# Seven products instead of eight in six more stages of a decoder trunk, with one PSUM bank per product

## The chip, the cores and the metric

The kernel runs on one core of a Trainium2 chip. Its time is the device time of one execution in microseconds; three executions before the change took 2046.9, 2049.47 and 2049.53 us, so the median is 2049.47 us. TensorE multiplies matrices into PSUM, VectorE (DVE in the profile) and ScalarE (ACT) do element-wise work, GpSimd (POOL) issues some of the transfers, SyncE (SP) issues the weight loads.

## The reference

One layer of a decoder for 256 tokens of width 2048, all in float32. A hybrid mixer runs three branches of width 1024 on the normalised input: differential attention (8 heads of two maps each), a causal convolution of 31 taps, and a chunked retention. Each branch result goes through its own 1024x2048 matrix, is multiplied by a sigmoid gate that is itself a 2048x2048 product, and the sum goes through `w_out`. Then comes cross-attention of 4 heads into 256 memory tokens (`w_q`, `w_kv`, `w_o`), then a SwiGLU feed-forward of width 5632 (`w_13`, `w_2`), each with a residual, and a last norm.

```python
h = rmsnorm(x, norm_mix)
x = x + hybrid_mixer(h, ...)                 # w_in: 18 blocks for the branches, 12 for the gates
x = x + cross_attention(rmsnorm(x, norm_xattn), rmsnorm(mem, norm_mem), wq, wkv, wo)
x = x + (silu(a) * b) @ w2                   # a, b = split(rmsnorm(x, norm_ffn) @ w13)
```

A block below is 512 output columns for all 256 tokens over the whole inner width; a weight chunk is 256 inner rows by 512 columns, half a megabyte.

## The kernel before

**Products in three parts.** Every weight chunk comes by one transfer from SP into a buffer of `raw` (10 of them). ACT rounds it to the short float format (`wh`, the high part, L198 to L199), DVE subtracts it from the chunk (`wl`, the low part, L201 to L202), and TensorE multiplies high by high, high by low and low by high (L286 to L288). `wh` and `wl` have 5 buffers each; a chunk's work is a unit, and the emitter makes the parts of up to 4 units ahead of the one whose products it emits (`LA`, L290 to L300). A unit of an ordinary block (`block`, L310) is 12 matmuls of 512 columns: two inner tiles, two token halves, three parts.

**The seven-product step.** `pair` (L388) takes two blocks with the same inputs. For the inner chunks marked S it splits the 2x2 arrangement of token halves and weight halves into seven products in place of eight (Strassen's scheme in Winograd's form): `quad_jobs` (L316) makes seven units of 6 matmuls where the ordinary way has four of 12. For this DVE adds weight halves into a raw buffer (`add`), POOL issues two accumulating transfers (L359, L375), and the inputs need four sums, `shi` and `slo`. Four of the seven products go to four PSUM banks of their own (`alloc_tp1`, L329) and are combined in `leave` (L404). Before the change this is used in ten pairs of the feed-forward stage, on two of the four inner chunks, twenty quads in all. The inputs there are normalised beforehand (`normalised`); elsewhere the row scale (`rsx`, `rsm`) is applied when a block leaves PSUM.

**What sets the order.** Attention, convolution, transposes and the like are generators, tasks; `pump` (L129) lets each of them take one step after each unit. Engine queues run in order. Instructions are placed by a scheduler with its own estimate of time, except those issued while `pin[0]` is set (L71 to L84), which keep the order in which the code wrote them, and the weight loads. While a pair's first part runs, `lock` stops all tasks that don't say 2.

Of the kernel before, what the change touches and what calls it, by code (L numbers as in the profile page):

```python
# [33 lines left out]
_CC = {}  # L34
# [6 lines left out]
LA = 4  # L41

# [13 lines left out]
def trunk(ctx, tc, xT, xtok, memT, memtok, w_in, w_br, w_out, w_q, w_kv, w_o, w_13, w_2,  # L56
# [7 lines left out]
    s4 = ctx.enter_context(tc.tile_pool(name="s4", bufs=27))  # L64
    sm = ctx.enter_context(tc.tile_pool(name="sm", bufs=4))
    tiny = ctx.enter_context(tc.tile_pool(name="tiny", bufs=12))
    psm = ctx.enter_context(tc.tile_pool(name="psm", bufs=2, space=bass.MemoryType.PSUM))
    pst = ctx.enter_context(tc.tile_pool(name="pst", bufs=4, space=bass.MemoryType.PSUM))
# [3 lines left out]
    class Pinned:  # L72


        def __init__(self, eng):
            self.eng = eng

        def __getattr__(self, name):
            f = getattr(self.eng, name)

            def g(*a, **k):
                i = f(*a, **k)  # L82
                return tc.keep_in_program_order(i) if pin[0] else i
            return g  # L84

    sc = Pinned(nc.scalar)
    ve = Pinned(nc.vector)
    pe = Pinned(nc.tensor)
# [25 lines left out]
    lock = [False]  # L114

    def spawn(gen):
        active.append(gen)
        return gen

    def step(g):  # L120
        try:
            said[g] = next(g)
# [5 lines left out]

    def pump():  # L129
        for g in list(active):  # L130
            if g in active and (not lock[0] or said.get(g) == 2):
                step(g)

    def drain(g):
        if g in active:
            assert not lock[0]
# [3 lines left out]
    def settle():  # L140

        for g in list(active):
            while g in active and said.get(g) == 1:
# [83 lines left out]
    def alloc_mm(ps):  # L227
# [62 lines left out]
    def emit_unit(i):  # L290
# [4 lines left out]
        for pr in u["prods"]:  # L295
            if pr[1] not in pr[0]:
                u["alloc"](pr[0])
# [18 lines left out]
    def quad_jobs(pp, ps0, ps1, w0, w1, a):  # L316
# [12 lines left out]
        def alloc_tp1(ps):  # L329
            for k in (1, 5, 6, 7):  # L330
                ps[k] = TP()
# [48 lines left out]
        def f4(u):  # L380
            parts(u, t.pop("a"))

        return ([unit(pp, 1, 0, 0, "n", f1, b11=w0[:, 0:2, :]),
                 unit(ps0, 0, 2, 0, "n", f2, b21=b21, b12=w1[:, 0:2, :]), unit(pp, 5, 0, 0, "s", f5),
                 unit(ps1, 0, 0, 3, "s", f3, b22=b22), unit(pp, 6, 0, 1, "s", f6)],
                [unit(pp, 7, 0, 2, "s", f7)], [unit(ps0, 1, 2, 1, "n", f4)])

    def pair(W0, W1, acts, modes, evac0, evac1):  # L388
# [15 lines left out]
        def leave():  # L404
            x0, x1 = S4([P, 2, 512]), S4([P, 2, 512])
            p1, u3, u4, v = x0[:, 0, :], x0[:, 1, :], x1[:, 0, :], x1[:, 1, :]
            sc.copy(p1, pp[1])

            ve.tensor_tensor(out=v, in0=pp[6], in1=p1, op=ALU.subtract)
# [1003 lines left out]
```

## Time and profile before

| | |
|---|---|
| median of three executions | 2049.47 us |
| the profiled execution | 2047.52 us |
| its span, first to last instruction | 2045.5 us |
| TensorE busy | 2021.5 us, 99% |
| VectorE busy | 1372.8 us, 67% |
| ScalarE busy | 1021.8 us, 50% |
| GpSimd busy | 54.8 us, 3% |
| weights and inputs read | 407.69 MB |

The shares are averages over the whole program. The stages differ: in the memory products VectorE is under half busy, in the convolution and attention part and in the feed-forward pairs it is mostly busy. The granted TensorE clock was 0.997 of full speed over the span.

### The profile page before, as it was taken

How to read it: one execution, taken by the hardware profiler on the slowest of the kernel's cores; microseconds unless marked ns; L12 is line 12 of the kernel's file. 1: busy time of each engine (PE TensorE's matmuls, PEld its weight loads, DVE VectorE, ACT ScalarE, POOL GpSimd, SP SyncE). 2: the span in 40 equal slices, each digit the busy share in tenths (PEclk: the TensorE clock that was granted, in tenths of full speed). 3: DMA queues.
4: the chain of work that ended last, by engine and by line, in shares of the span. 5: the costliest groups of instructions: out<-in, count | busy, mean ns of one | idle time of the engine just before them, and what ended most of it. 6: DMA issues, size and time to landing. Idle time of an engine off the chain costs nothing.

```text
span 2045.5 us, 24731 instructions
## 1 busy us (share of the span) xinstructions
PE 2021.5 (99%) x9253; PEld 1669.4 (82%) x9253; DVE 1372.8 (67%) x1684; ACT 1021.8 (50%) x1257; POOL 54.8 (3%) x72
## 2 busy tenths in 40 slices
PE   9999999999999999999999999999999999999998
PEld 6888888888888888888888888878788887888876
DVE  6995699776555556544455555588865888658874
ACT  7444444557544455444445544555543555435553
POOL 0000000000000000000000000000000000000100
PEclk9999999999999999999999999999999999999999
DMA  9656555554565666666655544548866788757881
GB/s 377 205 189 193 176 182 168 175 165 161 181 204 194 225 203 220 213 197 193 202 190 181 164 143 154 179 145 246 251 231 185 229 241 247 241 181 232 240 277 69
DMA packets 113879, 411.40 MB, mean 201 GB/s; under 512 B 12768, under 2 KB 13024, under 8 KB 113760
## 3 DMA queue, kind: packets, MB, share of 16 engines
q1 hardware_dynamic: 105552, 380.46, 54.9%
q0 software_dynamic: 8064, 29.36, 7.3%
q8 instruction: 72, 1.18, 0.2%
q14 instruction: 47, 0.39, 0.1%
q10 hardware_dynamic: 144, 0.01, 0.0%
HBM read 407.69 MB, written 2.10 MB: 200 GB/s over the span
## 4 chain that ended last, share of the span: by engine, by line
PE 84%; issue 6%; DMA 4%; DVE 3%; ACT 1%; POOL 0%; ACTq 0%; SPq 0%; POOLq 0%; DVEq 0%
PE mm L82 77%; PE tp L82 7%; DMA raw<-in_w 4%; DVE wl L82 2%; ACT wh L82 1%; DVE raw L82 1%; DVE s L82 1%; DMA raw<-in_w_in 0%; POOL raw L359 0%; ACT s L82 0%; SPq L90 0%; ACTq L1408 0%; ACTq L82 0%; POOLq L1408 0%; POOL rs L1275 0%
## 5 line engine op out<-in xcount | busy, mean ns | idle before, releaser
L82 PE MATMUL mm<-wh,s 128*128 128x512 f32 x5168 | 1632.0, 392 | 4.2 <-ACT wh L82 3.6
L82 DVE TENSOR_TENSOR wl<-raw,wh 128x1024 fp32r<-128x1024 f32 (+1 forms) x765 | 926.0, 1221 | 585.9 <-ACT wh L82 532.2
L82 ACT CAST wh<-raw 128x1024 fp32r<-128x1024 f32 (+1 forms) x765 | 793.4, 1051 | 831.1 <-PE mm L82 499.1
L82 PEld LDWEIGHTS mm<-wh,s 128*128 128x128 f32 x5168 | 970.0, 188 | 207.3 <-ACT wh L82 5.4
L82 PE MATMUL mm<-wl,s 128*128 128x512 f32 x2584 | 1009.5, 391 | 5.2 <-DVE wl L82 5.2
L82 PEld LDWEIGHTS mm<-wl,s 128*128 128x128 f32 x2584 | 485.9, 188 | 106.3 <-DVE wl L82 8.7
L82 PE MATMUL tp<-wh,s 128*128 128x512 f32 x384 | 130.7, 392 | 0.0
L82 DVE SCALAR_TENSOR_TENSOR s<-s,prm_t,s 128x256 fp32r<-128x256 f32 (+30 forms) x256 | 105.1, 466 | 0.0
L82 PEld LDWEIGHTS tp<-wh,s 128*128 128x128 f32 x384 | 72.7, 189 | 15.2
L82 DVE TENSOR_TENSOR s<-mm,s 128x1024 f32<-128x1024 f32 (+1 forms) x52 | 61.4, 1180 | 24.6 <-PE mm L82 24.6
L82 PE MATMUL tp<-wl,s 128*128 128x512 f32 x192 | 75.2, 392 | 0.0
L82 ACT ACTIVATE s<-s 128x512 f32<-128x512 f32 (+1 forms) x50 | 35.6, 713 | 75.7 <-DVE s L82 75.4
L82 DVE TENSOR_TENSOR s<-tp,s 128x512 fp32r<-128x512 f32 (+1 forms) x102 | 68.0, 685 | 7.3 <-PE tp L82 4.2
L82 DVE TENSOR_TENSOR s<-s,s 128x1024 f32<-128x1024 f32 (+4 forms) x68 | 66.3, 985 | 2.6 <-ACT s L82 1.3
L82 PE MATMUL tp<-cst_t,s 128*128 128x128 f32 x408 | 58.4, 273 | 5.3 <-ACT s L82 5.3
L82 PEld LDWEIGHTS tp<-cst_t,s 128*128 128x128 f32 x408 | 48.7, 140 | 17.5 <-ACT s L82 7.8
L82 PE MATMUL tp<-s,s 128*128 128x256 f32 (+4 forms) x340 | 52.7, 315 | 0.0
L82 PEld LDWEIGHTS tp<-s,s 128*128 128x128 f32 (+1 forms) x340 | 45.1, 189 | 6.4 <-issue 2.1
L82 DVE TENSOR_TENSOR raw<-raw,raw 128x1024 f32<-128x1024 f32 x40 | 48.9, 1222 | 0.6
L82 PEld LDWEIGHTS tp<-wl,s 128*128 128x128 f32 x192 | 36.3, 189 | 7.7
L82 ACT CAST s<-tp 128x512 fp32r<-128x512 f32 x58 | 32.7, 585 | 7.6 <-PE tp L82 7.6
L82 ACT ACTIVATE s<-mm,rsx 128x512 f32<-128x512 f32 x40 | 25.4, 687 | 20.2 <-PE mm L82 20.1
(77 smaller groups left out, 428.3 us busy)
## 6 DMA issues: line engine op xcount, KB each, us to landing
raw<-in_w SPq DMA_DIRECT2D x264, 512.0 KB, 5.1
raw<-in_w_in SPq DMA_DIRECT2D x239, 512.0 KB, 4.5
raw<-in_w_kv SPq DMA_DIRECT2D x64, 512.0 KB, 4.6
raw<-in_w_br SPq DMA_DIRECT2D x48, 512.0 KB, 4.3
raw<-in_w POOLq DMA_DIRECT2D x40, 512.0 KB, 8.3
raw<-in_w_out SPq DMA_DIRECT2D x32, 512.0 KB, 4.7
raw<-in_w_q SPq DMA_DIRECT2D x32, 512.0 KB, 4.2
raw<-in_w_o SPq DMA_DIRECT2D x32, 512.0 KB, 4.0
```

The source lines that it names most:

```text
L82: i = f(*a, **k)
```

## The change

The seven-product step is now used also in the differential-attention projections (three pairs, one S chunk of four, `MODES1`), the gates (six pairs), the memory keys and values (four), `w_out` (two), the last two blocks of `w_o` (one) and `w_2` (four), each with two S chunks of four (`MODES2`): 3 + 17 x 2 = 37 more quads. The block products of retention and the convolution stay ordinary, but take normalised inputs `xn`, as all of `w_in` does after its first two blocks.

The seven products of a pair now run product by product over its quads (p1 of both, p2 and p5 of both, p3 and p6 of both, p7, p4), each finished product leaves its bank at once (`join1` to `join7`), so a pair holds one bank at a time, and tasks run on while a pair runs, as long as no more than 3 banks are held (`cap`). Inside a pair ACT, DVE and TensorE keep the written order. Keys, values and the residual `x2` are parked in DRAM by transfers from POOL and loaded again when needed.

```diff
@@ pump and settle
-            if g in active and (not lock[0] or said.get(g) == 2):
+            if g in active and (said.get(g) or held() + wants[g] <= cap[0]):
                 step(g)
@@ quad_jobs
-        def alloc_tp1(ps):
-            for k in (1, 5, 6, 7):
-                ps[k] = TP()
+        def alloc_tp1(ps, key):
+            ps[key] = TP()
@@ pair
         def enter():
-            for c in sset:
-                need(acts[c])
-            settle()
+            settle(3)
+            cap[0] = 3
             pin[0] = True
-            lock[0] = True
...
+        def join1():
             x0, x1 = S4([P, 2, 512]), S4([P, 2, 512])
...
+            sc.copy(x0[:, 0, :], pp.pop(1))
+
+        def join5():
+            ve.tensor_tensor(out=xs[1][:, 1, :], in0=pp.pop(5), in1=xs[0][:, 0, :], op=ALU.add)
+
+        def join6():
+
+            p = pp.pop(6)
+            ve.tensor_tensor(out=xs[1][:, 0, :], in0=p, in1=xs[1][:, 1, :], op=ALU.subtract)
+            ve.tensor_tensor(out=xs[0][:, 1, :], in0=p, in1=xs[0][:, 0, :], op=ALU.subtract)
+
+        def join7():
+            p = pp.pop(7)
+            ve.tensor_tensor(out=xs[0][:, 1, :], in0=p, in1=xs[0][:, 1, :], op=ALU.subtract)
+            ve.tensor_tensor(out=xs[1][:, 1, :], in0=xs[1][:, 0, :], in1=p, op=ALU.subtract)
+            cap[0] = 4
...
+        first = units_of(("p1",), ("p2", "p5"), ("p3", "p6"))
...
+        us += mixed([marked(i, f) for i, f in enumerate(first)], n0)
+        us += [f() for f in units_of(("p7",))]
+        call(join7)
+        us += mixed(units_of(("p4",)), n1[:len(n1) // 2])
+        call(done(0, ps0, evac0))
         us += [f() for f in n1[len(n1) // 2:]]
+        call(done(1, ps1, evac1))
@@ inputs of the step
+    def factors(a, q):
+
+        f = S4([P, 4, 256])
...
+        for o, x, y, op in ((0, a22, a21, ALU.subtract), (2, a11, a21, ALU.subtract),
+                            (1, a22, fv[:, 2], ALU.add), (3, a12, fv[:, 1], ALU.subtract)):
+            ve.tensor_tensor(out=fv[:, o], in0=x, in1=y, op=op)
+        yield
+        a.shi, a.slo = S4([P, 4, 256], F32R), S4([P, 4, 256], F32R)
+        sc.copy(a.shi, f)
+        ve.tensor_tensor(out=a.slo, in0=f, in1=a.shi.bitcast(F32), op=ALU.subtract)
+
+    def whole(a):
+        q = S4([P, 4, 256])
+        ve.tensor_tensor(out=q, in0=a.hi.bitcast(F32), in1=a.lo.bitcast(F32), op=ALU.add)
+        return q
...
+    def times(q, rb):
+        ve.tensor_tensor(out=q, in0=q, in1=rb[:, None, :].broadcast_to([P, 4, 256]), op=ALU.mult)
@@ stages
+    diff_qk(0)
+    win(4, 5, MODES1, ev_dv(0), lambda ps: dst2[1].update(v=ps))
+    diff_qk(1)
...
+            win(18 + 4 * br + nb, 19 + 4 * br + nb, MODES2, ev_gate(nb), ev_gate(nb + 1))
...
+            pair(w0, w1, mm, MODES2, ev_kv(dst[h]), ev_kv(dst[h + 1]))
...
+        pair(w0, w1, mT, MODES2, ev1(nb), ev1(nb + 1))
...
+    pair(w0, w1, oT, MODES2, ev2(2), ev2(3))
...
+            pair(w0, w1, hT[lo:lo + 4], MODES2, ev_w2(nb), ev_w2(nb + 1))
@@ parking
+        def f(x):
+            nc.gpsimd.dma_start(out=dst, in_=x)
...
+            nc.gpsimd.dma_start(out=x2d[nb], in_=ps)
...
+            x2[nb] = S4([P, 2, 512])
+            nc.gpsimd.dma_start(out=x2[nb], in_=x2d[nb])
```

What moves, in two places. The first is one head of differential attention on DVE. Its score banks are `tp` (two maps), `tn` holds small statistics, the `128x2x128` row adds the causal mask, the last row of each map is the scaled maximum, and `s4_404` is the convolution, which runs beside it. Before:

```order
L82 TENSOR_TENSOR wl_583_3320<-raw_581_3317,wh_582_3319 128x1024
L82 TENSOR_TENSOR tp_566_3243<-tp_566_3243,cst_t_80 128x2x128
L82 TENSOR_TENSOR tp_567_3244<-tp_567_3244,cst_t_80 128x2x128
L82 TENSOR_REDUCE tn_572_3271<-tp_566_3243 128x1 x2
L82 TENSOR_SCALAR tn_572_3271<-tn_572_3271 128x2
L82 TENSOR_REDUCE tn_578_3304<-tp_567_3244 128x1 x2
L82 TENSOR_SCALAR tn_578_3304<-tn_578_3304 128x2
L82 RECIPROCAL tn_584_3337<-tn_571_3269 128x4
```

Now, a head in the third attention pair, on DVE again:

```order
L85 TENSOR_TENSOR tp_623_3427<-tp_623_3427,cst_t_82 128x2x128
L85 TENSOR_REDUCE tn_630_3450<-tp_623_3427 128x1 x2
L85 TENSOR_SCALAR tn_630_3450<-tn_630_3450 128x2
L85 TENSOR_TENSOR wl_633_3458<-raw_585_3235,wh_632_3457 128x1024
L85 SCALAR_TENSOR_TENSOR s4_404_2273<-s4_385_2170,prm_t_81,s4_404_2273 128x239
L85 SCALAR_TENSOR_TENSOR s4_404_2273<-s4_385_2170,prm_t_81,s4_404_2273 128x238
L85 TENSOR_TENSOR tp_624_3428<-tp_624_3428,cst_t_82 128x2x128
L85 TENSOR_REDUCE tn_634_3476<-tp_624_3428 128x1 x2
L85 TENSOR_SCALAR tn_634_3476<-tn_634_3476 128x2
L85 TENSOR_TENSOR wl_637_3484<-raw_577_3191,wh_636_3483 128x1024
```

The two maps of a head, together before, now stand in two successive steps, each followed at once by the low part of a weight chunk. On ACT at the same place stand the two exponentials of a map (`ACTIVATE`, into `sm`) and then the high part that this low part needs:

```order
L85 ACTIVATE sm_631_3454,tn_629_3448<-tp_623_3427,tn_630_3450 128x128
L85 ACTIVATE sm_631_3454,tn_629_3448<-tp_623_3427,tn_630_3450 128x256
L85 CAST wh_632_3457<-raw_585_3235 128x1024
L85 ACTIVATE sm_635_3480,tn_629_3448<-tp_624_3428,tn_634_3476 128x128
L85 ACTIVATE sm_635_3480,tn_629_3448<-tp_624_3428,tn_634_3476 128x256
L85 CAST wh_636_3483<-raw_577_3191 128x1024
```

The high part of the next chunk stands behind the exponentials that read the maximum; nothing else of DVE stands between that maximum and the low part.

The second place is TensorE at the change from one feed-forward pair to the next. `mm_1968` and `mm_2380` are results of a pair, `tp` a product's bank or a transpose's, `s4_1953` and `s4_2353` the gated hidden block of the pair before, which the four 128-column rows transpose. Before, in the later part of the next pair:

```order
L82 MATMUL mm_1968_10812<-wh_1997_10956,s4_1920_10614 128x512
L82 MATMUL mm_1968_10812<-wl_1998_10957,s4_1920_10614 128x512
L82 MATMUL mm_1968_10812<-wh_1997_10956,s4_1921_10615 128x512
L82 MATMUL tp_2014_11027<-cst_t_80,s4_1953_10774 128x128 x4
L82 MATMUL mm_1979_10859<-wh_2000_10968,s4_1954_10779 128x512
```

Now, right at the start of the next pair:

```order
L85 MATMUL mm_2380_11914<-wh_2404_12029,s4_2276_11444 128x512
L85 MATMUL tp_2421_12123<-wh_2407_12047,s4_2231_11256 128x512
L85 MATMUL tp_2421_12123<-wl_2408_12048,s4_2231_11256 128x512
L85 MATMUL tp_2421_12123<-wh_2407_12047,s4_2232_11257 128x512
L85 MATMUL tp_2421_12123<-wh_2407_12047,s4_2231_11256 128x512
L85 MATMUL tp_2421_12123<-wl_2408_12048,s4_2231_11256 128x512
L85 MATMUL tp_2421_12123<-wh_2407_12047,s4_2232_11257 128x512
L85 MATMUL tp_2424_12132<-cst_t_82,s4_2353_11802 128x128 x4
```

The transposes have come forward from after the seventh product of the next pair to after its first unit of six matmuls.

## Rows read from the trace of the kernel before

**Rows 1.** Page: span, busy time and share by engine, instructions.
```profile
span 2045.5 us, 24731 instructions
...
PE 2021.5 (99%) x9253; PEld 1669.4 (82%) x9253; DVE 1372.8 (67%) x1684; ACT 1021.8 (50%) x1257; POOL 54.8 (3%) x72
```
**Rows 2.** Stages: stretch, length, busy (x) PE PEld DVE ACT POOL, clock, DMA, GB/s.
```profile
920.00:980.00 60.00, 60.00 (x266) 49.69 (x265) 27.11 (x23) 26.65 (x28) 0.00 (x0) 1.00 0.60 192
```
**Rows 3.** The same columns: both attention groups, first gate block, second gate block.
```profile
283.60:432.40 148.80, 148.80 (x716) 122.53 (x715) 126.02 (x253) 68.53 (x101) 1.73 (x1) 1.00 0.53 172
432.40:458.30 25.90, 25.90 (x131) 21.13 (x130) 20.06 (x42) 16.34 (x34) 1.64 (x1) 1.00 0.51 164
...
471.80:497.10 25.30, 25.30 (x126) 20.55 (x125) 17.00 (x34) 23.82 (x41) 0.00 (x0) 1.00 0.44 145
```
**Rows 4.** The same columns: three feed-forward pairs.
```profile
1411.20:1454.30 43.10, 42.16 (x189) 34.41 (x188) 37.50 (x35) 23.47 (x26) 3.44 (x4) 1.00 0.79 239
1585.50:1626.30 40.80, 40.80 (x182) 33.78 (x181) 34.09 (x31) 24.02 (x24) 3.45 (x4) 1.00 0.83 246
...
1668.60:1712.60 44.00, 42.33 (x190) 34.45 (x189) 37.51 (x35) 24.13 (x27) 3.45 (x4) 1.00 0.80 239
```
**Rows 5.** VectorE in time: start, length, operation, count.
```profile
1413.46 1.22 DVE L82 TENSOR_TENSOR s<-mm,s 128x1024 f32<-128x1024 f32 x1
1414.71 1.23 DVE L82 TENSOR_TENSOR s<-s,s 128x1024 f32<-128x1024 f32 x1
1415.86 1.22 DVE L82 TENSOR_TENSOR raw<-raw,raw 128x1024 f32<-128x1024 f32 x1
1416.99 4.77 DVE L82 TENSOR_TENSOR wl<-raw,wh 128x1024 fp32r<-128x1024 f32 x4
```
**Rows 6.** Groups by line and shape on VectorE: count, busy us, mean ns.
```profile
L82 DVE TENSOR_TENSOR s<-tp,s 128x512 f32<-128x512 f32 x44 | 29.4, 687 | 5.6 <-PE tp L82 4.2
...
L82 DVE TENSOR_TENSOR s<-s 128x256 f32<-128x256 f32 x4 | 1.5, 419 | 0.0
```
**Rows 7.** ScalarE in time, one head of differential attention.
```profile
392.93 0.37 ACT L82 ACTIVATE sm<-tp,tn 128x128 f32<-128x128 f32 x1 [0.81 <-DVE tn L82]
...
393.74 0.37 ACT L82 ACTIVATE sm<-tp,tn 128x128 f32<-128x128 f32 x1
...
394.54 1.06 ACT L82 CAST wh<-raw 128x1024 fp32r<-128x1024 f32 x1
```
**Rows 8.** Who TensorE waited for: us in total, times, longest.
```profile
PE tp L82 <- ACT s L82: 5.3, 6, 2.1
PE mm L82 <- DVE wl L82: 5.2, 8, 2.1
PE mm L82 <- ACT wh L82: 3.6, 4, 1.9
```
**Rows 9.** Stretch in which the memory inputs are prepared, columns as before.
```profile
740.00:800.00 60.00, 60.00 (x275) 49.86 (x274) 38.81 (x48) 38.18 (x62) 2.83 (x5) 1.00 0.66 224
```
**Rows 10.** TensorE in time where the feed-forward pairs begin.
```profile
1371.07 0.51 PE L82 MATMUL mm<-wh,s 128*128 128x512 f32 x1 [1.85 <-ACT wh L82]
1373.65 0.79 PE L82 MATMUL mm<-wl,s 128*128 128x512 f32 x1 [2.08 <-DVE wl L82]
...
1375.52 0.63 PE L82 MATMUL mm<-wh,s 128*128 128x512 f32 x1
1375.95 0.63 PE L82 MATMUL tp<-wh,s 128*128 128x512 f32 x1
...
1379.87 0.39 PE L82 MATMUL mm<-wl,s 128*128 128x512 f32 x1
```
**Rows 11.** Transfers by issuing queue: count, KB each, median us to landing.
```profile
raw<-in_w SPq DMA_DIRECT2D x264, 512.0 KB, 5.1
...
raw<-in_w POOLq DMA_DIRECT2D x40, 512.0 KB, 8.3
```

More of the change, by code (lines that the diff above doesn't have):

```diff
@@ L121, in step @@
         try:
[L122 removed]
+            said[g] = next(g) or 0
             return True
@@ L135, in drain, with settle @@
         if g in active:
-            assert not lock[0]
+            settle(cap[0] - wants[g], g)
             while step(g):
                 pass
-    def settle():
-        for g in list(active):
-            while g in active and said.get(g) == 1:
+    def settle(n, keep=None):
+        while held() - said.get(keep, 0) > n:
+            g = next(g for g in active if said.get(g) and g is not keep)
+            while g in active and said.get(g):
                 step(g)
@@ new lines, in whole, with add_factors, spread @@
+    def whole(a):
+        q = S4([P, 4, 256])
+        ve.tensor_tensor(out=q, in0=a.hi.bitcast(F32), in1=a.lo.bitcast(F32), op=ALU.add)
+        return q
+    def add_factors(a):
+        yield from factors(a, whole(a))
+    def spread(st, rs):
+        dg = S4([P, 2, P])
+        on = S4([P, P])
+        ve.memset(on, 1.0)
+        for t in range(2):
+            ve.tensor_scalar(out=dg[:, t, :], in0=ident, scalar1=rs[:, t:t + 1], scalar2=None, op0=ALU.mult)
+        yield
+        tp = TP()
+        for t in range(2):
+            pe.matmul(tp[:, t * P:(t + 1) * P], on, dg[:, t, :], start=True, stop=True)
+        yield 1
+        rb = S4([P, 256])
+        sc.copy(rb, tp[:, 0:256])
+        tp = dg = on = None
+        st["rb"] = rb
@@ new lines, in times, with parts_task, normalise, chunk @@
+    def times(q, rb):
+        ve.tensor_tensor(out=q, in0=q, in1=rb[:, None, :].broadcast_to([P, 4, 256]), op=ALU.mult)
+    def parts_task(a, q):
+        a.hi, a.lo = S4([P, 4, 256], F32R), S4([P, 4, 256], F32R)
+        sc.copy(a.hi, q)
+        ve.tensor_tensor(out=a.lo, in0=q, in1=a.hi.bitcast(F32), op=ALU.subtract)
+    def normalise(src, dst, rs, sc=SC):
+        st = {}
+        freed = []
+        def chunk(c):
+            while len(freed) <= c:
+                yield
+            drain(st["task"])
+            q = whole(src[c])
+            times(q, st["rb"])
+            src[c].hi = src[c].lo = None
+            if c == 3:
+                st.pop("rb")
+            yield
+            parts_task(dst[c], q)
+            yield
+            if c in sc:
+                yield from factors(dst[c], q)
+        def after(c):
+            freed.append(c)
+            if c == 1:
+                rs()
+                st["task"] = spawn(spread(st, rs.tile))
+                for i in range(4):
+                    dst[i].task = spawn(chunk(i))
+        return after
@@ L996, in residual, with ev_kv, mT_factors @@
-    def residual(W, acts, xin, aT, gname, rs, parts, order=None):
+            mm[c].task = spawn(mem_chunk(c))
+    def ev_kv(dst):
+        def f(x):
+            nc.gpsimd.dma_start(out=dst, in_=x)
+        return f
+    def mT_factors():
+        for c in SC:
+            need(mT[c])
+            later(mT[c])()
+    for m, dst in ((0, kM), (4, vM)):
+        for h in (0, 2):
+            if m == 4 and h == 2:
+                call(mT_factors)
+            w0, w1 = ([w_kv[m + n, c] for c in range(4)] for n in (h, h + 1))
+            pair(w0, w1, mm, MODES2, ev_kv(dst[h]), ev_kv(dst[h + 1]))
```

411 lines of the change are left out of this document (213 added, 198 removed).

## The prediction

> **What bounds the kernel now.** I read the page's busy shares first, then busy time by stage, then single rows in time. TensorE is busy for 2021.5 of 2045.5 us [rows 1], and in a plain stretch its matmuls stand without a gap: 266 of 512 columns in 60 us, 225.6 ns each, at the full granted clock, while VectorE works less than half of the time (27.11 of 60 us) [rows 2]. So where VectorE has room, a matmul less is 225.6 ns less. VectorE doesn't have that room everywhere. In the differential-attention part it is busy for 126.02 of 148.8 us [rows 3], and in the feed-forward pairs, which already use seven products, for 34.09 of 40.8 to 37.51 of 44.0 us [rows 4]. There TensorE also begins to wait, up to 1.67 us in a pair (44.00 less 42.33). The reader is to see two kinds of stage: one in which TensorE alone sets the pace, and one in which the two engines are nearly level. The change takes work from TensorE and gives it to VectorE in both.
>
> **What it saves.** A quad has seven units of 6 matmuls in place of four of 12, so 6 fewer. There are 37 more quads: 222 matmuls, 222 x 225.6 ns = 50.1 us [rows 2]. All of it lies on the engine that sets the end, if that engine stays the bound. The Trainium skill, in TensorE: Matmul & The Clock Gate, section Back-to-back issue gap, gives N/2.4 + 2.5 ns for a matmul at the high clock, 215.8 ns for 512 columns; by that the saving would be 47.9 us. The trace has 225.6 ns, and the trace decides.
>
> **What it adds on VectorE.** Operations of 1024 columns that follow each other start 1.14 us apart (1415.86 to 1416.99 is 1.13, 1414.71 to 1415.86 is 1.15) [rows 5]; those of 512 columns take 0.69 us each [rows 6] and by the same overlap of 0.08 us cost some 0.6. A pair with two S chunks has 22 units in place of 16, so 6 more low parts, 4 additions of weight halves and 2 additions of parked sums: 12 x 1.14 = 13.7 us, and five joins of 512 columns, 3.0 us: 16.7 us. A pair with one S chunk has 3 + 2 + 2 = 7 of the long ones, 8.0 us, and the same joins: 11.0 us. The four sums for an S input are one whole (1.14), four of 256 columns (0.42 at most [rows 6], 0.34 by the overlap) and a low part (1.14): 3.6 us.
>
> **The memory, output and feed-forward stages.** Outside attention there is room for this: a block pair there takes 43.3 us of TensorE time (192 matmuls), of which VectorE now uses 43.3 x 27.11/60 = 19.6 us, and 16.7 on top gives 36.3 against 40.6 us (180 matmuls). That is how the present feed-forward pairs look, and the best of them takes 40.8 us [rows 4]; so I cost these pairs at their matmuls alone. Sums for the next stage's inputs (3.6 us a chunk, for `w_out`, `w_o` and four hidden blocks of the feed-forward) fall beside a pair too: 36.3 + 3.6 = 39.9 us still fits, by 0.7 us, and I cost them at nothing; without that cover they would be 3 us a pair. The normalising of the first inputs, four times three operations of 1.14 us, 13.7 us, and the parked values' loads lie beside ordinary blocks with half of VectorE free [rows 2], and their queue is POOL's, which is busy 3% [rows 1]. Where the memory inputs are prepared VectorE has 38.81 of 60 us [rows 9] and gets a pair, four multiplications by the row scale and two sets of sums: 38.8 + 16.7 + 4.6 + 7.2 = 67.3 us against 57.3 of TensorE; a lead of about 11 us (below) covers most, and I put 3 us there (0 to 7). Transfers: a feed-forward pair moves 16 chunks and 4 accumulations at a DMA share of 0.80 to 0.83 [rows 4]; the four pairs of `w_2` get two loads and two stores more, and 24/20 of 0.83 is 1.0. The four pairs may pay 0 to 2 us each; I take 2 us in all, since plain transfers are the lighter ones.
>
> **Attention and the first gates.** This decides. Both attention groups and two gate blocks had VectorE busy for 126.02 + 20.06 + 17.00 = 163.1 us in 148.8 + 25.9 + 25.3 = 200.0 us [rows 3]. The same work is now three one-chunk pairs and the first gate pair: 3 x 11.0 + 16.7 + 3.6 = 53.3 us more on VectorE, 216.4 us, while TensorE loses 30 matmuls and needs 193.2 us. VectorE is 23.2 us over. It may start ahead by 5 units, the number of `wh` buffers: 79 units in 193.2 us are 2.45 us each, 12.2 us of lead. That leaves 11 us.
>
> To this comes a wait that TensorE's slack covers today. In the new order the low part behind a map's maximum needs a high part that stands on ScalarE behind that map's two exponentials. These take 0.81 us (392.93 to 393.74) and the cast 1.06 us [rows 7], so VectorE stands for 1.87 us with nothing else in front of it: the next convolution step, the next map and the next sums all queue behind that low part. Eight heads of two maps give 16 x 1.87 = 29.9 us. As long as VectorE is ahead this costs nothing; in a stretch where it is behind, all of it does. Together 23.2 + 29.9 - 12.2 = 40.9 us. From below: the waits are covered by TensorE's own lateness, 11 us; from above: no lead is left at the start, 53 us. I take 40.9, since the balance is short even without the waits.
>
> **The pairs' seams.** The transposes of a pair's result now stand behind one unit of the next pair, 6 x 0.2256 = 1.35 us. Before them VectorE must add the parked sum (1413.46 to 1414.71) and multiply (1.23 us) [rows 5], 2.48 us from the last matmul, and a matmul's end lies 0.17 us behind the start of the next (0.39 - 0.2256 us, rows in time [rows 10]). TensorE waits 2.48 + 0.17 - 1.35 = 1.3 us. This happens at nine feed-forward seams, between the two pairs of `w_out`, and where a merged gate block meets a pair (two): 12 x 1.3 = 15.6 us. If VectorE is later at such a seam, 3 us each. Against that, the waits of transposes for a bank that ScalarE had to empty, 5.3 us in 6 places [rows 8], should go, since a pair holds one bank at a time.
>
> **Sum.** -50.1 + 40.9 + 15.6 - 5.3 + 3 + 2 = +6.1 us on the span of 2045.5 us. The profiled execution took 2047.52 us, 2.0 us more than its span and 1.95 us under the median of the three; I add to the median: 2049.5 + 6.1 = 2055.6, so 2056 us. The saving is real, and the attention part and the seams give it back.
>
> **Rivals.** First, VectorE keeps up: the waits behind the exponentials are hidden, attention costs 11 us and half of the seams 8: 2049.5 - 50.1 + 11 + 8 - 5.3 = 2013 us. For it: the same coupling stands in the profile today without a cost to TensorE, which is busy for all of those 148.8 us [rows 3]. Against it: the balance there was 15% in TensorE's favour and turns.
>
> Second, the clock falls. Where the feed-forward pairs begin, two waits of 1.85 and 2.08 us close to each other were followed by matmuls 0.43 us apart (1375.52 to 1375.95) in place of 0.2256, the lower of the two clock levels, from 1373.65 to 1379.87, some 13 of them: 2.7 us lost [rows 10]. If TensorE starved by VectorE sees that nine times in 240 us, it is 24 us more: 2080 us, slower, decided by whether waits come in clusters as there.
>
> Third, the accumulating transfers come late. POOL's land in 8.3 us against 5.1 for SP's [rows 11]. From the unit that issues one to the unit that needs it there are two ordinary units and three short ones, 2 x 2.71 + 3 x 1.35 = 9.5 us. With 114 more transfers on POOL's queue, stores among them that wait for VectorE, another 3.2 us would bring 11.5 us, and each of the 17 new two-chunk pairs would wait 2.0 us: 34 us, 2090 us. The Trainium skill, in SBUF — State Buffer, section SBUF: two separate sides, says that GpSimd can't write a transfer's descriptors while VectorE holds the port that they share, and names copies in VectorE's faster modes as what does this. The trace bears it out only so far as POOL's transfers are slower; how long VectorE held them no row shows.
>
> **Chances.** My forecast 0.50, with its own range of 2043 to 2073 us (attention 33 to 53, seams 10 to 22); VectorE keeps up 0.27; clock 0.13; late transfers 0.10. Two executions of this kernel differ by up to 0.13%, so within 0.2% (2045.4 to 2053.6 us) counts as no change. Of my forecast's half, 0.14 lies within that, 0.06 below and 0.30 above. The first rival is faster except for 0.03 that ends within; the others are slower. Faster 0.30, same 0.17, slower 0.53. The range has to reach to the first rival and to the clock's: 2010 to 2084 us leaves out some 0.11 of the first rival's chance below and 0.08 of the third's above.
>
> **What would show it.** Right: 222 fewer matmuls of 512 columns; between the first attention pair and the first gate blocks VectorE busy above 0.9 and TensorE idle for some 30 to 50 us, with waits of TensorE for `wl` and of VectorE for `wh`; waits of transposes for VectorE of about 1.3 us at the feed-forward seams; memory-product pairs of 40.6 to 41.5 us. Wrong: TensorE 99% busy there (then the first rival); stretches of the granted clock under 0.95 (the second); ScalarE waiting for `raw` from POOL in most pairs, or a DMA share at 1.0 in `w_2` (the third).

## The result and the profile after

The changed kernel takes 2180.36 us (median of four executions, 2176.44 to 2183.35), the kernel before 2049.5 us in the same series: the ratio is 1.064, 95% interval 1.0621 to 1.0659. It is slower, as forecast, but by 131 us and not by 6, far above the range. The page of the profiled execution, against [rows 1]:

```profile
span 2181.6 us, 25293 instructions
...
PE 2024.0 (93%) x9039; PEld 1655.9 (76%) x9039; DVE 1751.1 (80%) x2101; ACT 1131.9 (52%) x1363; POOL 142.6 (7%) x186
...
PE   9899998786899999899999999988999999999988
...
PEclk9899999897999999999999999999999999999999
```

The 222 matmuls are gone (6642 + 1464 of 512 columns in the groups `mm` and `tp`, 8106, for 8328). Yet TensorE is busy for 2024.0 us, not for 2021.5 - 50.1 = 1971.4, which is 52.6 us more. It is busy for 95.5 us at the lower clock, in 23 slow stretches, before for 5.8 us in 2; with matmuls 0.43 us apart there in place of 0.2256, that is an estimated 43 of the 52.6 us, and the other 10 were not taken apart. And TensorE stands still for 2181.6 - 2024.0 = 157.6 us, before for 24. So the saving of 50.1 us is there, and 186 us are lost beside it: 52.6 as longer busy time, most of it the clock, and some 134 as waits. A table by stage, each from its first matmul to the first of the next, in us, says where (the loss is after - before + the matmuls saved there at 0.2256; the 186.0 us between the first two rows and the end of the program are left out, for they did not change):

```
stage                                 before  after  saved   loss   no written order   best run
two first block pairs                   91.7  106.0    0.0   14.3        107.6            96.2
attention, first gate pair's blocks    226.7  301.1    6.8   81.2        255.1           226.2
gates up to the last pair              264.1  259.6   10.8    6.3        266.2           253.3
last gate pair and its branch blocks    67.1   80.1    2.7   15.7         65.9            65.7
memory pairs                           174.9  181.8   10.8   17.7        183.4           167.7
w_out to the first feed-forward pair   345.3  344.2    8.1    7.0        338.2           339.0
other feed-forward pairs and w_2       609.7  642.8   10.8   43.9        605.0           600.4
```

The stretches of [rows 3, 4] look like this after (stretch, length, busy (x) PE PEld DVE ACT POOL, clock, DMA, GB/s): the three pairs beside the heads, the first gate pair, the last gate pair with its branch blocks, a feed-forward pair, and the second pair of `w_2`.

```profile
297.60:484.60 187.00, 155.54 (x689) 123.28 (x688) 166.07 (x292) 75.86 (x107) 7.63 (x7) 0.92 0.48 147
484.60:574.80 90.20, 63.35 (x275) 48.27 (x274) 64.61 (x120) 46.41 (x84) 4.97 (x5) 0.81 0.46 128
...
858.30:938.40 80.10, 68.17 (x296) 55.53 (x295) 67.46 (x84) 47.70 (x71) 7.44 (x11) 0.94 0.71 223
...
1565.60:1612.90 47.30, 43.45 (x189) 35.70 (x188) 38.32 (x37) 25.53 (x28) 5.20 (x7) 0.96 0.81 244
1659.50:1700.30 40.80, 40.80 (x182) 33.78 (x181) 37.77 (x36) 23.15 (x23) 5.15 (x7) 1.00 0.93 309
```

The last row is what the change was to look like: 182 matmuls without a gap at the full clock, with VectorE busy for 37.77 of 40.80 us. Three gate pairs of the middle, at 40.8 us each, do this too. In the first gate pair neither engine is full (63.35 and 64.61 of 90.20 us): a stage bound by waits, not by work. TensorE's own waits (engine, for what: total us, times, longest), against [rows 8]:

```profile
PE tp L85 <- DVE s L85: 73.7, 25, 8.7
PE tp L85 <- DVE sm L85: 22.4, 11, 11.9
PE mm L85 <- ACT wh L85: 12.1, 4, 7.9
PE mm L85 <- ACT s L85: 12.0, 1, 12.0
PE tp L85 <- ACT sm L85: 11.5, 4, 8.4
```

Weights (`wh`, `wl`) are the smaller part of it. Most is transposes and head products, which stand in TensorE's queue in front of the next matmuls.

**Beside the heads.** VectorE and ScalarE in time, beside the first gate pair:

```profile
518.21 0.17 DVE L85 TENSOR_SCALAR tn<-tn 128x2 f32<-128x2 f32 x1
520.29 1.23 DVE L85 TENSOR_TENSOR wl<-raw,wh 128x1024 fp32r<-128x1024 f32 x1 [1.92 <-ACT wh L85]
```
```profile
505.48 1.28 ACT L85 ACT_TABLE_LOAD   x1
506.78 1.02 ACT L85 ACTIVATE s<-tp,prm_t 128x256 f32<-128x256 f32 x2
507.81 1.28 ACT L85 ACT_TABLE_LOAD   x1
...
518.41 0.37 ACT L85 ACTIVATE sm<-tp,tn 128x128 f32<-128x128 f32 x1 [1.90 <-DVE tn L85]
...
518.77 0.46 ACT L85 ACTIVATE sm<-tp,tn 128x256 f32<-128x256 f32 x1
...
519.22 1.04 ACT L85 CAST wh<-raw 128x1024 fp32r<-128x1024 f32 x1
```

ScalarE waits 1.90 us for the maximum, then makes two exponentials and the cast, and VectorE waits 1.92 us for that cast: the two take turns. The prediction had 1.87. Where the convolution's activations come between, a table load of 1.28 us (at 507.81) stands ahead of the exponentials and two copies, 1.07 us, behind them, and VectorE waits 4.04 us:

```profile
511.97 1.23 DVE L85 TENSOR_TENSOR wl<-raw,wh 128x1024 fp32r<-128x1024 f32 x1 [4.04 <-ACT wh L85]
```

From 297.6 to 598.7 us it waits 42.7 us for `wh`, in 27 places. The kernel before has such waits too, 28.5 us in 28 places from 283.3 to 510 us, but there TensorE never stands still.

**A seam.** Between the pair of the row 1565.60 and the next one, VectorE, ScalarE, TensorE:

```profile
1609.37 1.22 DVE L85 TENSOR_TENSOR s<-mm,s 128x1024 f32<-128x1024 f32 x1
1610.51 1.22 DVE L85 TENSOR_TENSOR raw<-raw,raw 128x1024 f32<-128x1024 f32 x1
1612.66 2.36 DVE L85 TENSOR_TENSOR wl<-raw,wh 128x1024 fp32r<-128x1024 f32 x2 [0.94 <-ACT wh L85]
1614.94 1.22 DVE L85 TENSOR_TENSOR s<-mm,s 128x1024 f32<-128x1024 f32 x1
1616.19 1.23 DVE L85 TENSOR_TENSOR s<-s,s 128x1024 f32<-128x1024 f32 x1
```
```profile
1610.63 1.06 ACT L85 ACTIVATE s<-s 128x1024 f32<-128x1024 f32 x1 [4.54 <-DVE s L85]
1611.60 3.96 ACT L85 CAST wh<-raw 128x1024 fp32r<-128x1024 f32 x4
```
```profile
1614.04 0.39 PE L85 MATMUL tp<-wh,s 128*128 128x512 f32 x1
1617.47 0.66 PE L85 MATMUL tp<-cst_t,s 128*128 128x128 f32 x4 [3.04 <-DVE s L85]
...
1620.01 0.63 PE L85 MATMUL mm<-wh,s 128*128 128x512 f32 x1
1620.43 0.63 PE L85 MATMUL mm<-wl,s 128*128 128x512 f32 x1
```

The last bank was full at 1613.07 (the matmul of 1612.68 and its 0.39 us). VectorE adds the parked sum only at 1614.94, behind two low parts, whose casts stand on ScalarE behind the activation, which stands behind the first sum. That is 1.9 us on top of the 1.3 us of the forecast, and behind the wait matmuls follow each other after 0.42 us in place of 0.2256.

### The profile page after: what moved, and what is told of

The parts are those of the page before. It is cut to its first block, busy times and chain, and to the rows that moved or that the text cites. A ratio compares the mean times of both kernels' runs of the same rounds, so it can differ in the third digit from the quotient of the medians.

```text
span 2181.6 us, 25293 instructions
## 1 busy us (share of the span) xinstructions
PE 2024.0 (93%) x9039; PEld 1655.9 (76%) x9039; DVE 1751.1 (80%) x2101; ACT 1131.9 (52%) x1363; POOL 142.6 (7%) x186
## 3 DMA queue, kind: packets, MB, share of 16 engines
q0 software_dynamic: 24480, 89.14, 20.1%
## 4 chain that ended last, share of the span: by engine, by line
PE 63%; DVE 16%; issue 10%; DMA 7%; ACT 3%; POOL 1%; ACTq 0%; SPq 0%; POOLq 0%; DVEq 0%
PE mm L85 50%; PE tp L85 13%; DVE s L85 7%; DVE wl L85 6%; DMA raw<-in_w 4%; ACT wh L85 2%; DVE raw L85 1%; DMA raw<-in_w_in 1%; DMA raw<-in_w_out 1%; DVE tn L85 1%; DMA raw<-in_w_kv 1%; ACT s L85 1%; DVE sm L85 0%; DMA raw<-in_w_o 0%; ACT sm L85 0%
## 5 line engine op out<-in xcount | busy, mean ns | idle before, releaser
L85 PE MATMUL mm<-wh,s 128*128 128x512 f32 x4428 | 1436.2, 396 | 28.7 <-ACT wh L85 12.1
L85 DVE TENSOR_TENSOR wl<-raw,wh 128x1024 fp32r<-128x1024 f32 (+1 forms) x876 | 1050.3, 1221 | 340.3 <-ACT wh L85 324.3
L85 ACT CAST wh<-raw 128x1024 fp32r<-128x1024 f32 (+1 forms) x876 | 897.1, 1050 | 696.2 <-PE mm L85 375.3
L85 PEld LDWEIGHTS mm<-wh,s 128*128 128x128 f32 x4428 | 844.7, 191 | 209.7 <-ACT wh L85 14.7
L85 PE MATMUL mm<-wl,s 128*128 128x512 f32 x2214 | 874.8, 395 | 8.7 <-DVE wl L85 8.7
L85 PE MATMUL tp<-wh,s 128*128 128x512 f32 x976 | 342.6, 401 | 0.0
L85 PEld LDWEIGHTS tp<-wh,s 128*128 128x128 f32 x976 | 188.2, 193 | 39.8 <-issue 0.5
L85 PE MATMUL tp<-wl,s 128*128 128x512 f32 x488 | 194.2, 398 | 0.4 <-DVE wl L85 0.4
L85 DVE TENSOR_TENSOR s<-tp,s 128x512 f32<-128x512 f32 (+1 forms) x182 | 120.9, 685 | 8.9 <-ACT s L85 4.3
L85 DVE SCALAR_TENSOR_TENSOR s<-s,prm_t,s 128x255 f32<-128x255 f32 (+23 forms) x256 | 112.1, 472 | 2.3
L85 ACT ACTIVATE s<-s 128x512 f32<-128x512 f32 (+1 forms) x62 | 48.4, 781 | 108.7 <-DVE s L85 94.5
L85 PEld LDWEIGHTS tp<-s,s 128*128 128x128 f32 (+1 forms) x348 | 46.5, 191 | 15.7 <-issue 10.5
```

## The experiments

All times are medians. The kernel before took 2048.08 to 2048.77 us in these series, the changed kernel 2180.36; its single executions lie up to 7 us apart, so 1 or 2 us are no difference. "Less" is against the changed kernel where nothing else is said. The names of stages are those of the table.

**The written order given up.**
```diff
-PIN = ("act", "dve", "pe")
+PIN = ()
```


> The changed kernel with the written order given up in the pairs: the scheduler sets the order on all three engines there. Coupling theory (in the written order a low part stands on VectorE behind a high part that stands on ScalarE behind the exponentials, so VectorE waited 42.7 us for high parts between 297.6 and 598.7 us, and TensorE idled 62 us there): most of these waits go, attention and first gates shorten by 35 to 60 us, and the feed-forward seams, where the same queue delays the multiplication, by 1 to 2 us each: 2085 to 2130 us. Rival, VectorE's work alone is too much there (230 us of work in 277 us): the order matters little, 2160 to 2185 us. Second rival: the written order is what keeps the seven-product pairs dense, and without it they get slower everywhere: over 2200 us.

2088.06 us, 92 less. The same matmuls; the three pairs beside the heads, the first gate pair, and a feed-forward pair:

```profile
299.20:453.50 154.30, 145.13 (x668) 117.39 (x667) 146.12 (x258) 72.87 (x95) 8.91 (x8) 0.98 0.63 186
453.50:529.50 76.00, 61.76 (x271) 46.69 (x270) 62.74 (x118) 49.80 (x81) 4.13 (x4) 0.91 0.46 140
...
1504.00:1545.70 41.70, 41.70 (x189) 34.61 (x189) 37.54 (x37) 25.23 (x26) 5.44 (x7) 1.00 0.90 278
```

These four pairs (the three beside the heads and the first gate pair) take 230.3 us for 277.2: 46.9 us were the order. They still take 37 us more than the 193.2 us of TensorE's work. VectorE is busy for 208.9 us of them, so its load alone accounts for 15.7 of the 37. TensorE stands still for 23.4 us, 16.0 of it for low parts and 2.4 for high parts, and is busy for 13.7 us longer, with the clock at 0.98 and 0.91. The third to the tenth feed-forward pair take 40.8 to 41.7 us (the one shown 41.7 for 47.3); the second and the last stay long, at 54.3 and 53.9. So the rival, that the order hardly matters, falls, and with it the second, that without it pairs get slower everywhere.

**Attention in ordinary blocks.**
```diff
-    MODES1 = "SNNN"
+    MODES1 = "NNNN"
-            dst2[g]["v"] = ps
+            dst2[g]["v"] = act(ps, AF.Identity, None)
```
(and the same for the other group's values)

> The changed kernel with ordinary blocks in place of the three one-chunk pairs of the differential attention; all other pairs stay. It has 18 matmuls more (4.1 us). From the start of these blocks to the end of the second pair of gate blocks the changed kernel takes 350 us, the kernel before 294. If the loss there comes from the attention's pairs (their VectorE work and the waits behind exponentials while they run), the stretch comes back by 50 to 70 us: 2110 to 2130 us. Rival, the loss comes from the first gate pair, beside which the second head group still runs (90 us in place of 49, 26.9 us of it idle): then only some 25 to 35 us come back, 2145 to 2155 us.

2130.77 us, 50 less. The three pairs' blocks take 147.9 us with TensorE busy for all of it; the first gate pair keeps its loss (87.0 us, 21.7 of it idle). The expectation and its rival both hold in part: 39 us came back beside the heads, and about as much is still lost in the first gate pair, beside which the second head group runs.

**Transposes three units later.**
```diff
+                for _ in range(3):
+                    yield
                 yield from transposed(hT[i], blk(s), None)
```
(and the same ahead of the transposes of residuals and merged gates)

> The changed kernel with the transposes of a pair's result put three units later (merged gates, residuals and hidden blocks). Seam theory: at some 12 seams TensorE waits 3 to 3.9 us for the multiplication and then runs 3.4 us at the lower clock, 1.5 us more; three short units, 4.1 us, cover the wait, and the clock stays up: 12 x 4.5 to 5.4 us less, 2115 to 2130 us. Rival, VectorE and ScalarE are late at the seam in any case (ScalarE stands for the first sum, VectorE behind its casts), so the wait moves to the next low part: 2165 to 2185 us.

2139.98 us, 40 less, where 50 to 65 were expected: the six feed-forward seams with a slow stretch gave 4.6 to 5.6 us each and the first memory pair 6.2, the other seams about 3 us or less. The third to the tenth feed-forward pair go to 40.8 to 43.4 us, in the written order. The rival (late in any case) falls.

**Eviction ahead of the normalising.**
```diff
-            while len(freed) <= c:
+            while len(freed) <= c or (c > 0 and len(freed) < 5):
...
         call(lambda: evac1(ps1["m"]))
+        call(lambda: after(4))
```


> The changed kernel with the preparation of the second to fourth normalised chunk held back until both banks of the two interleaved blocks (the first two blocks, and the first two of the feed-forward) are evicted. If the eviction that stands behind the normalising on ScalarE and VectorE is the cause of TensorE's 12.0 us wait at 53 us and of its 6.9 us wait at 1466 us, both go, with their slow-clock stretches (13.7 and 10.2 us at half speed): 15 to 25 us less, 2155 to 2165 us. Rival, the normalised chunks themselves are needed so soon that TensorE waits for them instead: within 6 us of 2180 us.

2178.13 us, no difference, where 15 to 25 were expected. TensorE's idle time in the first blocks fell from 13.7 to 7.5 us, but ahead of the second feed-forward pair it rose from 8.3 to 11.9. What it waited for in the changed kernel, TensorE and then ScalarE:

```profile
65.26 0.79 PE L85 MATMUL mm<-wh,s 128*128 128x512 f32 x1 [12.03 <-ACT s L85]
```
```profile
61.59 1.04 ACT L85 CAST s<-s 128x1024 fp32r<-128x1024 f32 x1 [3.69 <-DVE s L85]
62.65 1.28 ACT L85 ACT_TABLE_LOAD   x1
63.94 1.26 ACT L85 ACTIVATE s<-mm,rsx 128x512 f32<-128x512 f32 x2
```

The two interleaved blocks hold both accumulators; the sigmoid that empties one stands behind the casts of the normalised chunks. Holding these back won 5.3 us in the first blocks and lost 3.6 us in the second feed-forward pair, whose inputs then come later.

**The order on some engines only.**
```diff
-PIN = ("act", "dve", "pe")
+PIN = ("pe",)             # first run;  ("act", "dve") in the second
```


> The changed kernel with the written order kept on TensorE alone; VectorE and ScalarE are ordered by the scheduler. With no written order at all the time was 2088 us. If the loss in attention is VectorE's queue (low parts behind high parts behind exponentials) it goes here as it did there, 45 us; and if the loss at the feed-forward seams is the place of the transposes in TensorE's queue (behind one unit of six matmuls), it stays here, 3 to 5 us at each of some ten seams: 2120 to 2140 us. Rival, the seams too are VectorE's and ScalarE's order (second sum behind two low parts): then both go, 2085 to 2100 us.

> The changed kernel with the written order kept on VectorE and ScalarE, and given up on TensorE. By the theory of two places the seams come back, 40 to 45 us, and attention, a matter of VectorE's queue, stays as it was, 277 us for its four pairs: 2130 to 2145 us. Rival, TensorE's own order (the heads' transposes and products in front of matmuls that were ready) made the attention's loss: then attention comes back as well, 2090 to 2105 us. Second rival, the seams are the other engines' order: 2170 to 2185 us.

2167.25 us, 13 less, and 2178.92 us, no difference. The theory of two places fails in both. The first run's rival fails too; the second run's time lies in the range of its second rival (the seams are the other engines' order), but the first run, which frees these engines, contradicts that. Of the orders tried, only the one with all three engines free brought 92 us back. With TensorE alone written, the transposes still stand behind 6 matmuls and, from the third feed-forward pair on, wait 2.2 to 5.0 us. With TensorE free they go 31 matmuls into the next pair, and then ScalarE, which has their eviction at its old place, waits for them with the next casts behind it:

```profile
1564.41 0.59 ACT L85 CAST s<-tp 128x512 fp32r<-128x512 f32 x1 [5.01 <-PE tp L85]
...
1565.38 2.01 ACT L85 CAST wh<-raw 128x1024 fp32r<-128x1024 f32 x2
```

So at these seams a queue that keeps the early place holds the others. ScalarE or VectorE alone in the written order was not run.

**Loads to SP's queue, first blocks one behind the other** (no written order).
```diff
-            nc.gpsimd.dma_start(out=x2[nb], in_=x2d[nb])
+            ld(out=x2[nb], in_=x2d[nb])
...
-            us += half_jobs(ps0, [W0[c]], [acts[c]])
-            us += half_jobs(ps1, [W1[c]], [acts[c]])
+            us += half_jobs(ps0, [W0[c]], [acts[c]])
+        call(lambda: evac0(ps0["m"]))
+        for c in range(len(acts)):
+            us += half_jobs(ps1, [W1[c]], [acts[c]])
```
(the residual inputs' and the gains' loads likewise)

> No written order, and two more edits at separate places. The plain loads of the residual inputs, the parked sums and the final gains go to SP's queue; if it was these, ahead of an accumulation in POOL's queue, that made TensorE wait 6.3 us in the last memory pair and 9.2 us in the last feed-forward pair, these waits go: 8 to 11 us and 11 to 13 us. And the two first blocks stand behind each other, no longer interleaved, so that one bank is evicted while the other block runs: the waits for an eviction, 12 to 14 us at the start and 10 us ahead of the second feed-forward pair, go with their slow stretches, 20 to 25 us in all; if instead the normalised inputs are late, half of that. Sum: 2040 to 2050 us, from 2088. Rival, the accumulations are late for another reason (the chip's transfers are full there): 2060 to 2068 us.

2079.31 us, 9 less than without the order; 38 to 48 were expected. Three of four places answered: the last memory pair went from 51.7 to 43.7 us, the last feed-forward pair from 53.9 to 41.7, the first blocks from 107.6 to 95.2. The second feed-forward pair stayed (55.6), and the second pairs of `w_2` went from 40.8 to 48.4 and 52.1 us: there the moved loads stand in SP's queue ahead of weights (ahead of the first of these pairs SP waits 14.8 us for the loads' buffer and 7.6 us for the store of a parked sum before it goes on with weights). What the accumulations had waited behind, in the changed kernel, POOL's queue and then ScalarE:

```profile
2066.85 1.41 POOL L1388 DMA_DIRECT2D s<-in_gfin  x2
2067.93 2.42 POOL L1407 DMA_DIRECT2D s<-x2d  x4
2072.12 0.88 POOL L383 DMA_DIRECT2D raw<-in_w  x1 [1.77 <-DVE wl L85]
```
```profile
2093.56 5.94 ACT L85 CAST wh<-raw 128x1024 fp32r<-128x1024 f32 x6 [15.26 <-DMA raw<-in_w]
```

Six loads of half a megabyte went in ahead, and the accumulation landed 21 us after its issue; the median is 8.1. The Trainium skill, in DMA: Bandwidth & Descriptors, section SWDGE vs HWDGE vs iDMA, sends plain transfers to SP or ACT and leaves accumulating ones to GpSimd. By that all these loads move; the trace agrees for the loads at the end (53.9 to 41.7 us), and not for those of `w_2` (40.8 to 48.4 and 52.1).

**All repairs, seven products left out beside the heads and in the first gate pair** (on top of the run before).
```diff
-    MODES1 = "SNNN"
+    MODES1 = "NNNN"
-            win(18 + 4 * br + nb, 19 + 4 * br + nb, MODES2, ...)
+            win(18 + 4 * br + nb, 19 + 4 * br + nb, MODES0 if bi + nb == 0 else MODES2, ...)
```


> As the run with SP loads and separate first blocks, and the differential attention and the first gate pair in ordinary blocks (30 matmuls more, 6.8 us). With no pair beside the heads VectorE has room, and the 230 us that the three attention pairs, the first gate pair and its branch blocks took without the written order become some 205 to 212 us: 2015 to 2030 us, under the kernel before. Rival, the last accumulations and the inputs of the memory stage keep their waits: 2035 to 2055 us, no gain over the kernel before.

2041.97 us, ratio to before 0.9972 (0.996 to 0.9984), which is what the rival gave. The blocks of the four pairs took 200.2 us, with TensorE busy for all of it, and 226.2 with the branch blocks; the 230 us of the expectation had been the four pairs alone, so its 205 to 212 was held against the wrong stretch. With the loads in SP's queue the second pairs of `w_2` took 50.5 and 49.8 us.

**Exponentials one unit later, all else written.**
```diff
                 ve.tensor_scalar(out=mx, in0=mx, scalar1=-0.125, ...)
+                yield 2 - m
                 e = SM(384)
```


> The changed kernel, all in its written order, with one edit: between the maximum of a map of the differential attention and its two exponentials stands one more unit, so that the casts of the next unit stand ahead of the exponentials on ScalarE, and no low part waits for a high part behind a maximum that VectorE has only just made. VectorE's work is the same. Coupling theory: the four pairs, 277 us in the changed kernel and 230 us without the written order, shorten by 25 to 45 us: 2135 to 2155 us. Rival, in the written order it is TensorE's place of the heads' transposes and products, which wait for the softmax's results, that costs: less than 12 us, 2168 to 2182 us.

2151.02 us, 29 less; the four pairs take 252.0 us for 277.2. There ScalarE's waits for a maximum fall from 42.6 to 14.3 us, VectorE's for high parts from 38.2 to 20.1, and TensorE's for results or banks of the softmax from 33.4 to 20.5. The instructions are the same, so 25 us were the turns that VectorE and ScalarE took: the coupling costs that much by itself. How it reaches TensorE, by its waits for the softmax, is told below.

**Written order, repaired.** The edits of the runs before (exponentials, transposes, loads of residual inputs, gains and last sums, first blocks) in one kernel, with the feed-forward's inputs normalised from the end of its first block.

> The written order kept, all pairs as in the changed kernel, and four repairs: exponentials one unit later, transposes of results three units later, the residual inputs', gains' and last parked sums' loads in SP's queue, the two first blocks (of the kernel and of the feed-forward) one behind the other, with the feed-forward's inputs normalised from the first block's end. If the places in the written order and the two queues are the whole loss beyond VectorE's work, some 30 + 40 + 20 + 22 us come back of 131: 2060 to 2075 us, and what is left of the loss against the kernel before lies in the four pairs beside the heads (35 to 45 us) and in the memory stage. Rival, written order keeps other waits: 2090 to 2110 us.

2086.95 us: 93 less, 12 above the expected range. The four pairs stay at 253.1 us, the second feed-forward pair at 53.8, the last gate pair at 56.9.

**The best version.** As the run with all repairs, with the feed-forward's inputs normalised from the end of its first block, the parked sums of `w_2` loaded by POOL again, and
```diff
+            if m + h == 0:
+                for n in (0, 1):
+                    block(w_kv, n, mm, ev_kv(dst[n]))
+                continue
             pair(w0, w1, mm, MODES2, ev_kv(dst[h]), ev_kv(dst[h + 1]))
...
-    call(lambda: load_x2(range(4)))
+    call(lambda: load_x2(range(4), ld))
```


> No written order; the differential attention, the first gate pair and the first memory pair in ordinary blocks (42 matmuls more than the changed kernel, 9.5 us); the two first blocks one behind the other, and the feed-forward's inputs normalised from its first block's end; the residual inputs, the gains and the last parked sums loaded by SP's queue, the other parked sums again by POOL's. Against the run with all repairs: the two second pairs of the last weights, 50.5 and 49.8 us there, go back to 41 (19 us less), the second feed-forward pair from 55.7 to 42 to 46 us, the first memory pair from 51.5 to 44 to 46 us: 2003 to 2015 us, 35 to 45 us under the kernel before. Rival, the normalising is late however early it starts, and the memory inputs too: 2016 to 2026 us.

2015.49 us, ratio to before 0.9838 (0.9824 to 0.9852): less than both kernels, by 33 and 165 us, and half a us above the expected range. The first memory pair took 45.3 us, the second feed-forward pair 55.0: the earlier normalising did not help there.

**The waits filled** (the changed kernel again).
```diff
+                for i in range(fill if pr == 0 else 0):
+                    pe.matmul(tq, wz[:, 0:P], wz, start=True, stop=True)
...
-                yield from transposed(hT[i], blk(s), None)
+                yield from transposed(hT[i], blk(s), None, 12)
```


> The changed kernel with 12 matmuls of zeros, 512 columns each, 2.7 us in all, in front of the first transposes of each of the ten hidden blocks that a pair follows; nothing waits for them, and they stand where TensorE waited 3.0 to 3.9 us in six seams. They don't shorten the wait for the multiplication. If the slow-clock stretch of 3.4 us behind these six waits comes from TensorE's standing still, it goes, and each of these pairs takes 1.3 to 1.7 us less (45.5 to 46 us for 47.2 to 47.4), while the fifth feed-forward pair, which waited only 1.2 us, gets 1.5 us longer: 2165 to 2175 us in all, and six to eight slow stretches fewer of the 23. Rival, the clock falls there for another reason, and the fill costs where it is longer than the wait: 2180 to 2186 us.

2172.05 us, 8 less, with 120 matmuls more. The seam shown above, and its pair:

```profile
1607.60:1652.00 44.40, 44.40 (x201) 35.58 (x200) 40.66 (x39) 24.75 (x26) 4.57 (x6) 1.00 0.84 249
```
```profile
1608.97 2.76 PE L85 MATMUL tp<-wz 128*128 128x512 bf16 x12
...
1612.32 0.39 PE L85 MATMUL tp<-wl,s 128*128 128x512 f32 x1
1612.55 0.62 PE L85 MATMUL tp<-wh,s 128*128 128x512 f32 x2
```

The clock stays at 1.00, matmuls stand 0.23 us apart behind the transposes, and 16 slow stretches are left of 23; the six behind the feed-forward seams are among those that went. The pairs behind these seams take 1.4 to 2.2 us less. So the fall at these seams comes from TensorE's standing still.

## Why the prediction was wrong, step by step

**Right.** 222 matmuls fewer, 50.1 us of work; the place that loses most (attention and first gates); the turns of VectorE and ScalarE there, with 1.92 us for the 1.87 of one; the wait of the transposes at the seams; pairs without a seam in front at 40.8 us with the sums beside them; `w_2` not slowed by its extra transfers (its second pairs take 40.8 us). That the change made the kernel slower was forecast by 6 us and with a chance of 0.53; the direction came out right, but more by luck than by the sum.

**The step that failed** is "Together 23.2 + 29.9 - 12.2 = 40.9 us". The stage lost 81.2, and by another path. In the prediction VectorE's lateness reaches TensorE as late low parts, "with waits of TensorE for `wl`". TensorE's waits from 297.6 to 598.7 us:

```profile
PE tp L85 <- DVE sm L85: 22.4, 11, 11.9
PE tp L85 <- DVE s L85: 19.5, 7, 6.2
PE tp L85 <- ACT sm L85: 11.0, 3, 8.4
PE mm L85 <- DVE wl L85: 2.2, 2, 1.2
```

Low parts are 2.2 us of it. The rest is transposes and products for the heads and the convolution: they wait for results of VectorE, those of the softmax above all, or for a bank that the softmax still reads, as one of TensorE's rows in the first gate pair shows:

```profile
504.09 1.12 PE L85 MATMUL tp<-cst_t,s 128*128 128x128 f32 x4 [8.41 <-ACT sm L85]
```

TensorE's queue is written too, so they stand in front of its next matmuls. The sum had no term for this. It let the wait of one engine stand alone; here three queues in one fixed order hand each wait on, as the two runs with a part of the order showed. The lead of 12.2 us that it took off was a lead in low parts, and TensorE hardly waited for these.

The sizes: the four pairs take 277.2 us for 193.2 us of TensorE's work, 84.0 more (the branch blocks behind them win 2.8 back). Of this 46.9 us went with the written order, where 29.9 stood, and moving the exponentials alone gave back 25. The other 37 us stay without the written order, where 23.2 - 12.2 = 11 stood. There the path is the forecast one: TensorE stands still for 23.4 us, 18.4 of it for low and high parts, and is busy for 13.7 us longer, at clocks of 0.98 and 0.91, for which the sum had nothing.

**The seams** were priced at 1.3 us, 15.6 in all. In the seam shown TensorE waits 3.04 us; at nine feed-forward seams, from the third pair on, the transposes wait 27.6 us in all, where 9 x 1.3 = 11.7 stood, and putting them later gave back 40 us with the clock. The sentence "If VectorE is later at such a seam, 3 us each" was the likely case: VectorE's queue between the two sums holds two low parts that wait for ScalarE, which the forecast of 1.3 us left out. Of the waits for a bank that ScalarE had to empty, 5.3 us, 2.6 us stayed.

**The clock** was a rival with 0.13, as a matter of clusters of waits. Its sign, a clock under 0.95, shows in three of the stretches above (0.92, 0.81, 0.94). It was no rival but came with the forecast's own waits: an estimated 43 us of slower matmuls on some 134 us of waits, 0.3 us for each on average. Had the 40.9 + 15.6 + 3 us of waits been right, that would have been some 19 us more, by the same estimate. The Trainium skill, in TensorE: Matmul & The Clock Gate, section HAM oscillation, describes waits that recur between pieces of work, each followed by a start at half rate; the trace agrees, with 23 slow stretches for 2, but not for every wait, as the last section shows.

**What stood at nothing or little.** The normalised inputs "beside ordinary blocks" cost 14.3 us at the start (12.0 of it one wait): the eviction was queued behind them, with both accumulators held. The memory stage stood at 3 us and lost 15.7 + 17.7: in the last gate pair a wait of 8.7 us of the small matmul that spreads the row scale (gone without the written order, where the pair took 44.1 us for 57.5), in the last memory pair ScalarE's wait of 8 us for an accumulation behind two plain loads. The third rival, late accumulations, was right at two places (the last memory pair and the last feed-forward pair) and for a reason it did not name: plain loads ahead in the same queue. Moving these shortened both.

**Open** is the second feed-forward pair, 49.8 us before and 52.2 to 57.4 us in all runs, 55.0 in the best: starting the normalising earlier, evicting first and separating the blocks each left it. How much of the 37 us beside the heads is late accumulations was not tried; without the written order ScalarE waited 3.4, 10.3 and 5.6 us for one there.

## What to carry to other kernels

Before adding work to an engine that still has room on average, write down, for the queue of each engine around the place, what stands ahead of the instruction that the bottleneck waits for, and go around the circle once: where two engines hand results back and forth in a fixed order, their times add. Do this for the bottleneck's own queue too: here the waits were for transposes and small products in it, not for weights. A wait on TensorE can be paid again in slow matmuls, here an estimated 0.3 us for each microsecond on average. And use a step that trades one engine's time for another's only where the other is idle in that very stage: leaving it out in five of the twenty new pairs, with the order left to the scheduler, the first blocks one behind the other and some loads moved to SP's queue, turned 131 us lost into 33 us won.

## What the runs showed of the hardware that was not expected

Waits that look alike differ in what follows. The seam of 3.04 us above was followed by a slow stretch, one of 3.01 us near the end of the changed kernel by none (the wait, and the pair's row with its clock of 1.00):

```profile
2012.46 0.66 PE L85 MATMUL tp<-cst_t,s 128*128 128x128 f32 x4 [3.01 <-DVE s L85]
```
```profile
2007.90:2052.90 45.00, 41.99 (x189) 34.49 (x188) 40.01 (x38) 25.83 (x27) 3.61 (x5) 1.00 0.84 237
```

Why they differ stays open. Twelve matmuls of zeros in short floats, 2.76 us, in front of such a wait kept the clock at 1.00. An accumulating transfer behind six plain ones in the same queue landed after 21 us, where the median is 8.1.
